# A two-layer trunk: modulation sums spread over other stages, the first head's inputs copied early, one norm per head

## The chip, the core and the metric

The kernel runs on one core of a Trainium2 chip. TensorE (PE) multiplies matrices and transposes tiles into PSUM, VectorE (DVE) and ScalarE (ACT) work on tiles and read PSUM, GpSimd (POOL) takes some work beside them, and SyncE's queue (SP) issues most of the transfers, in order. The metric is the time of one execution on the device in microseconds. The kernel before took 1466.41 us, the median of three runs (1465.34 to 1467.45).

## What is computed

A trunk of two layers over 1024 tokens of width 1024, in float32. Layer 0 is a gated delta rule in 8 heads, layer 1 is stick-breaking attention in 16 heads over keys and values that are computed once between the layers. Each layer's input is normed and modulated by vectors from `c`; the norm for keys and values has vectors of its own.

```python
for layer in range(DEPTH):
    mod = c_act @ w_ada[layer] + b_ada[layer]
    shift, scale, gate = mod[:, :D], mod[:, D:2 * D], mod[:, 2 * D:]
    h = _modulated_norm(x, norm_g[layer], shift, scale)
    if layer < N_A:
        y = _gdn_mixer(h, w_in_a[i], conv_w_a[i], a_log_a[i], dt_bias_a[i], o_gain_a[i], w_out_a[i])
    else:
        if layer == N_A:
            mkv = c_act @ w_ada_kv + b_ada_kv
            hk = _modulated_norm(x, kv_norm_g, mkv[:, :D], mkv[:, D:])
            kv = hk @ w_kv
...
        y = _sb_mixer(h, k_sh, v_sh, w_in_b[i], q_gain_b[i], w_out_b[i])
    x = x + (gate[:, None, :] * y).astype(x.dtype)
```

In the mixer of layer 0, queries, keys and values are projected, pass a causal convolution of four taps and a silu, queries and keys are normed, and a recurrence over chunks of 64 tokens runs per head. `beta` and the decay `g` ("the gates" below) come from 16 more columns of the projection. The recurrence's output is normed per head, multiplied by a silu of `z` and projected back.

## The kernel before

The work lies in four stages, and TensorE is the engine that all others feed.

**Start (0 to 78 us).** `x` is normed and transposed, the shift and scale of layer 0 are made, and the tokens times the gates' columns and the first head's queries go into PSUM (`ba_ps`, `q_ps`, L343 and L344). Then a block in which TensorE's order is that of the code (L439 to L497) projects the first head's keys into two banks (`pk0`), makes the gates from `ba` (sigmoid, exponentials, logarithm and a series, on tiles of 128x64 in a pool of their own, `gt`), sums them over the chunk with two matmuls (`pgc`, L484, L485), and transposes the sums (`pgt`, L493), which are written to memory and read back on all partitions.

**Heads (78 to 700 us).** `conv_silu` (L502) projects a head's queries or keys (for the first head it takes the finished ones out of PSUM), copies them from PSUM to `xp` (L512) and, scaled by one tap, to `qk` (L513), adds three taps on VectorE (L515) and applies the silu (L517). Each projection is three matmuls per block: every float32 operand is a high and a low half (`mm3`, L116 to L118; the weight's halves are `whi`, a cast on ScalarE, L211, and `wlo`, a subtract on VectorE, L212). `stage_qk` transposes (`ptk`, L543), squares (L545) and norms queries and keys, decays the keys (`kdec`, L549), makes the products of the chunk (`pgr`, L576) and inverts a triangular matrix row by row (L603, L606); `stage_c` (L688) runs the recurrence and norms its output, for each half of the tokens by a chain of 13 small VectorE operations (L735, L736 and `rsqrt`, L91). The loop over heads (L747) issues the next head's `stage_qk` ahead of the current head's rest. A scheduler orders the instructions of this stage, apart from the blocks said above to follow the code.

Two vectors of layer 0's and the key/value norm's and three of layer 1's are still missing: `mods` (L527) lists six pairs of matrix and part. After each of the heads 0 to 5, `mod_acc` (L145) sums one of them: sixteen loads of 256 KB (`mraw`) and sixteen VectorE operations on 128x512 (`macc`, L153, L155), and in the next head `mod_fin` (L170) transposes the sums (`pc`, L182) and adds them up by two ScalarE instructions for each transpose (L185).

**Keys and values (700 to 945 us).** The rest of layer 0 and the projection of keys and values, in TensorE's hand-written order (L947 on). `keys_values` goes through eight column blocks `n`, four of keys and then four of values, each in two halves of four steps; a step is 24 matmuls on 256 columns. After each block `mod_b(n)` (L919) reads a part of the normed `x`, modulates it for layer 1 on ScalarE and splits it into halves, the low one by GpSimd (L927).

**Layer 1 (945 us to the end).** Queries, attention and the last projection; the change does not touch it.

Of the kernel before, what the change touches and what calls it, by code (L numbers as in the profile page):

```python
# [17 lines left out]
EPS = 1e-6  # L18
# [4 lines left out]
def kernel(  # L23
# [146 lines left out]
    def mod_fin(pool, ps_pool, ps_tag, i, part, accs, j0=0, turned=False):  # L170

        t = pool.tile([P, ND], F32, name="mt", tag="mt", bufs=2)
# [262 lines left out]


    k_ps = [dd_pool.tile([P, 512], F32, name="pk0", tag="dd"), o_pool.tile([P, 512], F32, name="pk0", tag="po")]
    with tc.tile_pool(name="gt", bufs=1, side="right", reuse_waits="tile") as gt:
        order = tc.manual_schedule(engines={PE.engine})  # L439
        order.__enter__()  # L440
        ba = gt.tile([P, T], F32, name="ba")
# [10 lines left out]
        alb = gt.tile([P, 2, HA], F32, name="alb")  # L452
# [3 lines left out]
        y = gt.tile([P, HA, NC], F32, name="gy")  # L456
        V.tensor_tensor(out=y, in0=pbv[:, 8:16, :], in1=alb[:, 1, :][:, :, None].broadcast_to([P, HA, NC]),
                        op=ALU.add)
        u = gt.tile([P, HA, NC], F32, name="gu")
        V.scalar_tensor_tensor(out=u, in0=y, scalar=-1.0, in1=y, op0=ALU.mult, op1=ALU.min)  # L460
        S.activation(out=u, in_=u, func=AF.Exp)
        ea = gt.tile([P, HA], F32, name="ea")
        S.activation(out=ea, in_=alb[:, 0, :], func=AF.Exp)
        w1 = gt.tile([P, HA, NC], F32, name="gw1")
        S.activation(out=w1, in_=u, func=AF.Ln, bias=1.0)

        sr = gt.tile([P, HA, NC], F32, name="gsr")
# [6 lines left out]
        mk = gt.tile([P, HA, NC], F32, name="gmk")  # L474
# [19 lines left out]
        gT = gt.tile([64, P], F32, name="gT")  # L494
        V.tensor_copy(out=gT, in_=pgt[:64, :P])
        dma(out=gTd, in_=gT)
        order.__exit__(None, None, None)  # L497

    gdn_stack = ctx.enter_context(ExitStack())
    gp = gdn_stack.enter_context(tc.tile_pool(name="gp", bufs=1, side="right", reuse_waits="tile"))  # L500

    def conv_silu(h, part, dst):  # L502
        j = part * 8 + h
        ready = {0: q_ps, 8: k_ps}.get(j)
        if not ready:
            hi, lo = split_w(load_w(w_in_a[0][:, j * P:(j + 1) * P]), [P, ND, P], None, V)
        xp = gp.tile([P, 3 + T], F32, name="xp", tag="xp", bufs=2)
        V.memset(xp[:, 0:3], 0.0)
        for hf in range(TH):
            ps = ready[hf] if ready else project(hi, lo, hT, hf)  # L510
            sl = slice(hf * 512, hf * 512 + 512)
            S.copy(out=xp[:, 3 + hf * 512:515 + hf * 512], in_=ps)  # L512
            S.activation(out=dst[:, sl], in_=ps, func=AF.Copy, scale=ccol[:, 72 + j:73 + j])  # L513
# [13 lines left out]
    mods = [(0, 2), (2, 1), (2, 0), (1, 1), (1, 0), (1, 2)]  # L527

    def stage_qk(h):

        qk = gp.tile([P, 2, T], F32, name="qk", tag="qk", bufs=3)
# [156 lines left out]
    def stage_c(h, st):  # L688
# [37 lines left out]
        for hf in range(TH):  # L726
            cs = slice(hf * 4, hf * 4 + 4)
            osb = osbs[hf]
            so = gp.tile([P, 4], F32, name="so", tag="so")
            for i in range(4):  # L730
                sqo = gp.tile([P, P], F32, name="sqo", tag="sqo")
                S.activation(out=sqo, in_=osb[:, i], func=AF.Square, accum_out=so[:, i:i + 1])

            qe = gp.tile([P, 4], F32, name="qe", tag="qe")
            V.tensor_scalar(out=qe, in0=n2[:, 0, cs], scalar1=EPS, scalar2=EPS * P, op0=ALU.add, op1=ALU.mult)  # L735
            V.scalar_tensor_tensor(out=so, in0=so, scalar=1.0 / P, in1=qe, op0=ALU.mult, op1=ALU.add)  # L736
            ro = rsqrt(gp, so, 4, "ro")
            V.tensor_tensor(out=osb, in0=osb, in1=ro[:, :, None].broadcast_to([P, 4, P]), op=ALU.mult)
            pt = ch_pool.tile([P, 4, P], F32, name="pto", tag="ch")
            for i in range(4):  # L740
                PE.transpose(pt[:, i], osb[:, i], ident)
            V.scalar_tensor_tensor(out=szs[hf], in0=pt.rearrange("p a b -> p (a b)"), scalar=ogain,
                                   in1=szs[hf], op0=ALU.mult, op1=ALU.mult)
            dma(out=oTa[h, :, hf * 512:hf * 512 + 512], in_=szs[hf])
# [4 lines left out]
    for h in range(HA):  # L749
# [169 lines left out]
    def mod_b(n):  # L919
# [360 lines left out]
```

## Time and profile before

| | |
|---|---|
| median of three runs | 1466.41 us (1465.34 to 1467.45) |
| the profiled execution | 1462.12 us |
| its span | 1460.3 us |
| mean granted clock of TensorE | 0.985 of full |
| TensorE, VectorE, ScalarE, GpSimd busy | 1374.8, 1040.8, 760.6, 92.3 us |

A granted clock of 1 is 2.4 GHz, and 0.5 is 1.2 GHz; a stretch between the two has part of its time at each. Matmuls overlap, so the pace of a stream is read from the starts of two neighbours, and the time of one is longer than that. In brackets behind an instruction stands the idle time of its engine just ahead of it and what ended that.

### The profile page before, as it was taken

How to read it: one execution, taken by the hardware profiler on the slowest of the kernel's cores; microseconds unless marked ns; L12 is line 12 of the kernel's file. 1: busy time of each engine (PE TensorE's matmuls, PEld its weight loads, DVE VectorE, ACT ScalarE, POOL GpSimd, SP SyncE). 2: the span in 40 equal slices, each digit the busy share in tenths (PEclk: the TensorE clock that was granted, in tenths of full speed). 3: DMA queues.
4: the chain of work that ended last, by engine and by line, in shares of the span. 5: the costliest groups of instructions: out<-in, count | busy, mean ns of one | idle time of the engine just before them, and what ended most of it. 6: DMA issues, size and time to landing. Idle time of an engine off the chain costs nothing.

```text
span 1460.3 us, 23391 instructions
## 1 busy us (share of the span) xinstructions
PE 1374.8 (94%) x8603; PEld 1145.8 (78%) x8603; DVE 1040.8 (71%) x2459; ACT 760.6 (52%) x1614; POOL 92.3 (6%) x98
## 2 busy tenths in 40 slices
PE   4989999799999999999799999999999999998998
PEld 3567778578878777788689999788888888885676
DVE  3568698878778788954886610488888888989332
ACT  5656546446564646431784422366666666665110
POOL 1000000000000000000221011301011011000000
PEclk9999999799999999999999999999999999999999
DMA  9334324443444444444844433624233233234511
GB/s 316 107 107 124 89 51 120 123 137 84 142 108 133 108 137 134 148 127 162 301 160 159 160 131 116 181 73 116 54 101 106 69 105 87 84 84 131 174 59 56
DMA packets 168132, 181.15 MB, mean 124 GB/s; under 512 B 36617, under 2 KB 121426, under 8 KB 168018
## 3 DMA queue, kind: packets, MB, share of 16 engines
q1 hardware_dynamic: 165184, 171.17, 39.4%
q0 software_dynamic: 2432, 8.39, 1.6%
q8 instruction: 68, 1.11, 0.3%
q14 instruction: 46, 0.38, 0.1%
q10 hardware_dynamic: 402, 0.10, 0.0%
HBM read 140.22 MB, written 39.40 MB: 123 GB/s over the span
## 4 chain that ended last, share of the span: by engine, by line
PE 70%; DVE 18%; ACT 6%; DMA 3%; issue 2%; SPq 0%; ACTq 0%; DVEq 0%
PE pj L116 16%; PE pj L117 16%; PE pj L118 16%; DVE kp L1074 3%; PE ptw L1089 3%; PE pa L1114 2%; PE pa L1115 2%; PE pl L1069 1%; PE pl L1068 1%; PE pgr L576 1%; DVE qk L515 1%; DVE wl L1096 1%; DVE macc L155 1%; DMA mraw<-in_w_ada_dram 1%; PE pa L1111 1%
## 5 line engine op out<-in xcount | busy, mean ns | idle before, releaser
L118 PE MATMUL pj<-hT,wlo 128*128 128x512 f32 x496 | 203.0, 410 | 10.2 <-DVE wlo L212 10.2
L116 PE MATMUL pj<-hT,whi 128*128 128x512 f32 x496 | 205.4, 414 | 3.7 <-ACT qk L513 2.6
L117 PE MATMUL pj<-hT,whi 128*128 128x512 f32 x496 | 204.5, 412 | 0.0
L1074 DVE TENSOR_TENSOR_SCAN kp<-kp,stick 128x896 f32<-128x896 f32 (+7 forms) x128 | 179.1, 1401 | 3.9 <-ACT kp L1070 2.6
L1070 ACT ACTIVATE kp<-pl,nrq 128x512 f32<-128x512 f32 (+1 forms) x192 | 107.0, 580 | 48.6 <-PE pl L1069 39.9
L1094 ACT ACTIVATE wh<-ptw 128x512 fp32r<-128x512 f32 (+3 forms) x152 | 84.6, 557 | 67.4 <-PE ptw L1089 63.2
L118 PEld LDWEIGHTS pj<-hT,wlo 128*128 128x128 f32 x496 | 95.2, 192 | 27.6 <-DVE wlo L212 11.8
L116 PEld LDWEIGHTS pj<-hT,whi 128*128 128x128 f32 x496 | 95.2, 192 | 24.2 <-issue 3.7
L116 PE MATMUL pj<-hbT,whi 128*128 128x512 f32 x256 | 108.0, 422 | 0.0
L117 PEld LDWEIGHTS pj<-hT,whi 128*128 128x128 f32 x496 | 95.3, 192 | 15.8
L116 PE MATMUL pj<-wo,oh 128*128 128x512 f32 x256 | 103.8, 405 | 4.0 <-ACT oh L254 2.3
L117 PE MATMUL pj<-wo,oh 128*128 128x512 f32 x256 | 102.1, 399 | 0.0
L118 PE MATMUL pj<-wo,ol 128*128 128x512 f32 x256 | 101.3, 396 | 0.5 <-DVE ol L255 0.5
L117 PE MATMUL pj<-hbT,whi 128*128 128x512 f32 x256 | 101.2, 395 | 0.0
L118 PE MATMUL pj<-hbT,wlo 128*128 128x512 f32 x256 | 101.2, 395 | 0.0
L1089 PE MATMUL ptw<-ident,kp 128*128 128x128 f32 x576 | 91.6, 277 | 8.1 <-DVE wl L1096 5.5
L212 DVE TENSOR_TENSOR wlo<-wraw,whi 128x1024 fp32r<-128x1024 f32 x56 | 68.7, 1226 | 39.8 <-ACT whi L211 35.5
L211 ACT CAST whi<-wraw 128x1024 fp32r<-128x1024 f32 x56 | 59.1, 1055 | 72.1 <-PE pj L117 61.0
L1096 DVE SCALAR_TENSOR_TENSOR wl<-ptw,wh 128x512 fp32r<-128x512 f32 (+1 forms) x140 | 87.3, 624 | 8.1 <-ACT wh L1094 7.2
L1089 PEld LDWEIGHTS ptw<-ident,kp 128*128 128x128 f32 x576 | 68.4, 142 | 27.3 <-DVE wl L1096 12.0
L1114 PE MATMUL pa<-wh,vt 128*128 128x256 f32 (+1 forms) x280 | 78.5, 302 | 10.6 <-DVE o L1131 10.6
L116 PE MATMUL pj<-whi,hkT 128*128 128x256 f32 x256 | 73.2, 286 | 2.4 <-DVE x L265 1.6
(324 smaller groups left out, 3428.8 us busy)
## 6 DMA issues: line engine op xcount, KB each, us to landing
mraw<-in_w_ada_dram SPq DMA_DIRECT2D x96, 256.0 KB
wraw<-in_w_in_a_dram SPq DMA_DIRECT2D x32, 512.0 KB
mraw<-in_w_ada_kv_dram SPq DMA_DIRECT2D x32, 256.0 KB
xr<-x_dram SPq DMA_DIRECT2D x16, 512.0 KB
wraw<-in_w_kv_dram SPq DMA_DIRECT2D x16, 512.0 KB
kT_dram<-kt SPq DMA_DIRECT2D x32, 256.0 KB
wraw<-in_w_in_b_dram SPq DMA_DIRECT2D x16, 512.0 KB
Kh<-kT_dram SPq DMA_DIRECT2D x32, 256.0 KB
```

What stands on the lines that cost most here:

```text
L116: PE.matmul(ps, lh, rh, start=start, stop=False)
L117: PE.matmul(ps, lh, rl, start=False, stop=False)
L118: PE.matmul(ps, ll, rh, start=False, stop=stop)
L211: (copy or S.copy)(out=hi, in_=raw)
L212: (eng or G).tensor_tensor(out=lo, in0=raw, in1=hi, op=ALU.subtract)
L1070: S.activation(out=kp[:, s0:s0 + sw], in_=pl[:, :sw], func=AF.Sigmoid, scale=nrq[p][:, t, e:e + 1])
L1074: V.tensor_tensor_scan(out=kr, data0=kr, data1=stick[:, T - n:][:, ::-1], initial=1.0, op0=ALU.mult, op1=ALU.max)
L1089: PE.transpose(pt[:, i], kps[p, e, 2 * g + q][:, j * P:(j + 1) * P], ident)
L1094: S.activation(out=wh[:, :nb], in_=pt[:, :nb], func=AF.Copy, bias=-1.0)
L1096: V.scalar_tensor_tensor(out=wl[:, :nb], in0=pt[:, :nb], scalar=-1.0, in1=wh[:, :nb], op0=ALU.add, op1=ALU.subtract)
L1114: PE.matmul(dst, lh, wh[:, sl], start=(j == 0), stop=False)
L1115: PE.matmul(dst, lh, wl[:, sl], start=False, stop=(j == nj - 1))
```

## The change

1. The first head's queries and keys are copied from PSUM (`taps_in`) inside the gates' block, the queries ahead of the gates, each half of the keys behind its projection; `conv_silu` then finds them in `first_xp` and `first_qk`. The gates' tiles are pieces of one tile in the heads' pool, which is opened earlier. The block in which TensorE follows the order of the code stays; later work can still come in between.
2. `mods` keeps three pairs, and each of the heads 0 to 5 sums one half of one. Layer 1's three vectors are summed in the stage of keys and values, in twelve quarters of 256 columns (four loads of 256 KB and eight VectorE operations on 128x256 each), which begin at the steps `MOD_Q`, counted from block 4 on; a quarter is transposed four steps after it began.
3. `mod_b` goes from the end of each block to the steps `MOD_B`, and its low half is made by VectorE.
4. `stage_c` norms both halves of the tokens by one chain, but in the last head.

```diff
-    def mod_fin(pool, ps_pool, ps_tag, i, part, accs, j0=0, turned=False):
+    def mod_quarters(pool, i, part):
+
+        for n0 in range(0, D, 256):
+            src = mod_src[i][:, part * D + n0:part * D + n0 + 256].rearrange("(p k) n -> p k n", k=8)
+            acc = pool.tile([P, 256], F32, name="macq", tag=("of", "oh", "ol")[n0 // 256 % 3], bufs=2)
+            for k in range(0, 8, 2):
+                raw = pool.tile([P, 2, 256], F32, name="mrawq", tag="x2k", bufs=5)
+                dma(out=raw, in_=src[:, k:k + 2])
...
-        else:
+        elif js.stop == ND:
             pr = ps_pool.tile([P, 512], F32, name="pr", tag=ps_tag)
             PE.transpose(pr[:ND, :P], t, ident)
...
+    def taps_in(j, ps, hf, xp, dst):
+
+        S.copy(out=xp[:, 3 + hf * 512:515 + hf * 512], in_=ps)
+        S.activation(out=dst[:, hf * 512:hf * 512 + 512], in_=ps, func=AF.Copy, scale=ccol[:, 72 + j:73 + j])
...
+        for hf in range(TH):
+            taps_in(0, q_ps[hf], hf, first_xp[0], first_qk[:, 0])
...
         for hf in range(TH):
             project(hi, lo, hT, hf, k_ps[hf])
+            taps_in(8, k_ps[hf], hf, first_xp[1], first_qk[:, 1])
...
-    mods = [(0, 2), (2, 1), (2, 0), (1, 1), (1, 0), (1, 2)]
+    mods = [(0, 2), (2, 1), (2, 0)]
+    half_acc = []
...
+        groups = [(0, 1)] if h < HA - 1 else [(0,), (1,)]
+        for group in groups:
+            ga = slice(group[0] * 4, group[-1] * 4 + 4)
...
+            ro = rsqrt(gp, so[:, ga], 4 * len(group), f"ro{len(group)}")
...
-        if h < len(mods):
-            i, part = mods[h]
-            pend = (i, part, [mod_acc(gp, i, part, n0, 512, 2) for n0 in (0, 512)])
+        if h < 2 * len(mods):
+            i, part = mods[h // 2]
+            half_acc.append(mod_acc(gp, i, part, h % 2 * 512, 512, 2))
+            if h % 2:
+                pend, half_acc = (i, part, half_acc), []
...
-            G.tensor_tensor(out=hT[hf][:, 1, n], in0=xs, in1=hT[hf][:, 0, n], op=ALU.subtract)
+            V.tensor_tensor(out=hT[hf][:, 1, n], in0=xs, in1=hT[hf][:, 0, n], op=ALU.subtract)
...
+    def mods_b(step, made):
+
+        if quarters and quarters[0][0] + 4 <= step:
+            _, i, acc, j0 = quarters.pop(0)
+            mod_fin(kp_, wk_pool, "wk", 1, (1, 0, 2)[i], [acc], j0, tg if i == 2 else None, turned=True)
+        if step in MOD_Q:
+            n = MOD_Q.index(step)
+            quarters.append((step, n // 4, *next(made)))
...
+                    if n >= 4:
+                        mods_b(step, made)
+                        if step in MOD_B:
+                            mod_b(MOD_B.index(step))
+                        step += 1
                     yield
...
-            mod_b(n)
+    MOD_Q = (0, 1, 3, 4, 6, 7, 9, 10, 16, 19, 22, 25)
+    MOD_B = (15, 16, 18, 19, 21, 22, 24, 26)
```

ScalarE's order at the first head, before: `gu` and `gw` belong to the gates, `pgc` are their sums in PSUM, `pj` and `pk` the first head's queries and keys there.

```order
L465 ACTIVATE gw_681<-gu 128x64
L211 CAST whi<-wraw 128x1024
L490 ACT_TABLE_LOAD
L490 ACTIVATE gA_110<-pgc 128x64
L491 ACTIVATE gA_109<-gA_109 128x64
L512 COPY xp<-pj 128x512
L513 ACTIVATE qk<-pj,ccol 128x512
L512 COPY xp<-pj 128x512
L513 ACTIVATE qk<-pj,ccol 128x512
L512 COPY xp<-pk_597 128x512
L513 ACTIVATE qk<-pk_597,ccol 128x512
L512 COPY xp<-pk_598 128x512
```

And with the change, where `gsm` is the gates' tile:

```order
L478 COPY ba<-pba 128x512 x2
L457 COPY xp<-pj 128x512
L458 ACTIVATE qk<-pj,ccol 128x512
L457 COPY xp<-pj 128x512
L458 ACTIVATE qk<-pj,ccol 128x512
L493 ACT_TABLE_LOAD
L493 ACTIVATE gA_111<-pb 128x64
L501 ACT_TABLE_LOAD
L501 ACTIVATE gsm<-gsm 128x8
L633 COPY tt<-tinit 128x256
L227 CAST whi<-wraw 128x1024
L457 COPY xp<-pk_603 128x512
```

The copies of the queries have moved from behind the gates' last exponentials to ahead of their first (`pb`, the sigmoid); the first half of the keys (`pk_603`) follows its projection, ahead of the rest of the gates, and so does the second further down.

TensorE behind the keys of the first head (`pgc`: the gates' sums, `pj`: the second head's queries), before and, from that projection's seventeenth matmul, with the change:

```order
L117 MATMUL pk_598<-hT,whi 128x512
L118 MATMUL pk_598<-hT,wlo 128x512
L484 MATMUL pgc<-gw_681,tri 128x64
L485 MATMUL pgc<-gw_681,ones 128x64
L493 MATMUL pgt<-ident,gA_108 64x128
L116 MATMUL pj<-hT,whi 128x512
L117 MATMUL pj<-hT,whi 128x512
```

```order
L117 MATMUL pj<-hT,whi 128x512
L118 MATMUL pj<-hT,wlo 128x512
L116 MATMUL pj<-hT,whi 128x512
L117 MATMUL pj<-hT,whi 128x512
L522 MATMUL pgc<-gsm,tri 128x64
L523 MATMUL pgc<-gsm,ones 128x64
L118 MATMUL pj<-hT,wlo 128x512
L116 MATMUL pj<-hT,whi 128x512
L117 MATMUL pj<-hT,whi 128x512
L118 MATMUL pj<-hT,wlo 128x512
L116 MATMUL pj<-hT,whi 128x512
L531 MATMUL pgt<-ident,gA_108 64x128
```

The gates' sums and their transpose stood ahead of the second head's first projection (`pj`); with the change that projection follows the keys at once, and the sums come after twenty of its matmuls.

SyncE's queue at the eight quarters that come first, with the change, behind the last loads of the stage's weights:

```order
L177 DMA mrawq<-in_w_ada_dram 128x2x256 x5
L233 DMA wraw<-in_w_kv_dram 128x4x256
L177 DMA mrawq<-in_w_ada_dram 128x2x256
L233 DMA wraw<-in_w_kv_dram 128x4x256
L177 DMA mrawq<-in_w_ada_dram 128x2x256 x2
L958 DMA kT_dram<-kt 128x512 x3
L177 DMA mrawq<-in_w_ada_dram 128x2x256
L958 DMA kT_dram<-kt 128x512
L177 DMA mrawq<-in_w_ada_dram 128x2x256 x7
L941 DMA v_dram<-kv 128x4x128
L942 DMA v_dram<-kv 4x1x128
L941 DMA v_dram<-kv 128x4x128
```

And TensorE at the last quarter:

```order
L118 MATMUL pj<-kwh,hkT 128x256
L198 MATMUL pc<-ident,macq 128x128 x2
L218 MATMUL pr<-ident,tg 8x128
L116 MATMUL pj<-whi,hkT 128x256
L117 MATMUL pj<-wlo,hkT 128x256
```

Quarters' loads, two weights (`wraw`), the last key tiles (`kT_dram`) and the first values (`v_dram`) share the queue; on TensorE, `pr` is the very next instruction after the last quarter's transposes.

## Rows read from the trace of the kernel before

**Rows 1.** The page, part 1: busy us, share of the span, instructions.

```profile
PE 1374.8 (94%) x8603; PEld 1145.8 (78%) x8603; DVE 1040.8 (71%) x2459; ACT 760.6 (52%) x1614; POOL 92.3 (6%) x98
```

**Rows 2.** Busy time by stretch (busy us and instructions per engine, granted clock, DMA share, GB/s).

```profile
core 0: us, PE busy (x) PEld busy (x) DVE busy (x) ACT busy (x) POOL busy (x), PEclk, DMA share, GB/s
...
78.00:88.00 10.00, 7.02 (x22) 5.40 (x21) 4.74 (x10) 7.70 (x15) 0.00 (x0) 0.66 0.56 162
88.00:258.00 170.00, 167.34 (x1023) 135.25 (x1022) 143.83 (x442) 99.89 (x215) 0.00 (x0) 1.00 0.36 98
258.00:282.00 24.00, 13.89 (x45) 9.32 (x44) 23.24 (x87) 10.83 (x28) 0.00 (x0) 0.65 0.43 120
282.00:475.00 193.00, 191.06 (x1265) 155.42 (x1264) 151.18 (x493) 107.41 (x271) 0.00 (x0) 1.00 0.44 121
475.00:484.00 9.00, 6.03 (x23) 4.52 (x22) 9.00 (x30) 7.15 (x13) 0.00 (x0) 0.81 0.50 134
484.00:700.00 216.00, 209.51 (x1333) 169.32 (x1331) 154.57 (x483) 93.98 (x231) 1.46 (x3) 1.00 0.46 142
...
800.00:900.00 100.00, 100.00 (x858) 100.00 (x857) 34.22 (x59) 35.98 (x69) 14.23 (x10) 1.00 0.41 134
```

**Rows 3.** TensorE's waits, 100 to 700 (us in total, times, longest).

```profile
PE pj L118 <- DVE wlo L212: 10.2, 4, 5.4
PE pgr L576 <- ACT kdec L549: 3.2, 2, 1.6
```

**Rows 4.** TensorE's timeline at the first head (start us, us, instruction, idle before).

```profile
81.97 0.80 PE L116 MATMUL pj<-hT,whi 128*128 128x512 f32 x1 [2.57 <-ACT qk L513]
...
87.66 0.40 PE L117 MATMUL pj<-hT,whi 128*128 128x512 f32 x1
87.89 0.40 PE L118 MATMUL pj<-hT,wlo 128*128 128x512 f32 x1
...
93.29 1.09 PE L543 MATMUL ptk<-ident,qk 128*128 128x128 f32 x8 [1.15 <-ACT qk L517]
```

**Rows 5.** ScalarE's timeline at the first head.

```profile
78.13 1.04 ACT L211 CAST whi<-wraw 128x1024 fp32r<-128x1024 f32 x1 [6.90 <-PE pk L117]
...
80.75 0.58 ACT L512 COPY xp<-pj 128x512 f32<-128x512 f32 x1
...
82.27 0.72 ACT L513 ACTIVATE qk<-pj,ccol 128x512 f32<-128x512 f32 x1
```

**Rows 6.** TensorE's timeline, 255 to 285.

```profile
267.15 2.07 PE L576 MATMUL pgr<-qk 128*128 128x256 f32 x4 [1.61 <-ACT kdec L549]
...
276.04 0.79 PE L118 MATMUL pj<-hT,wlo 128*128 128x512 f32 x1 [5.39 <-DVE wlo L212]
```

**Rows 7.** VectorE's timeline, 247 to 283.

```profile
262.20 0.75 DVE L155 SCALAR_TENSOR_TENSOR macc<-mraw,cact,macc 128x512 f32<-128x512 f32 x1
...
274.77 1.21 DVE L212 TENSOR_TENSOR wlo<-wraw,whi 128x1024 fp32r<-128x1024 f32 x1
```

**Rows 8.** Groups of VectorE, 78 to 700 (busy us, mean ns, idle before).

```profile
L155 DVE SCALAR_TENSOR_TENSOR macc<-mraw,cact,macc 128x512 f32<-128x512 f32 x84 | 62.6, 745 | 6.3 <-DMA mraw<-in_w_ada_dram 4.5 <-DMA mraw<-in_w_ada_kv_dram 1.5
...
L101 DVE SCALAR_TENSOR_TENSOR ro_y<-ro_z,ro_y 128x4 f32<-128x4 f32 x48 | 7.5, 156 | 0.4
...
L153 DVE TENSOR_SCALAR macc<-mraw,cact 128x512 f32<-128x512 f32 x12 | 5.8, 481 | 9.5 <-ACT macc L185 9.5
```

**Rows 9.** The sums' groups on ScalarE and TensorE, 78 to 700.

```profile
L185 ACT ACTIVATE macc<-pc 128x128 f32<-128x128 f32 x48 | 12.5, 286 | 8.2 <-PE pc L182 8.2
...
L185 ACT ACTIVATION_READ_ACCUMULATOR macc<-pc 128x1 f32 x48 | 10.4, 217 | 0.0
...
L182 PE MATMUL pc<-ident,macc 128*128 128x128 f32 x48 | 7.3, 275 | 0.0
```

**Rows 10.** The DMA view, 0 to 40.

```profile
DMA packets 7758, 12.43 MB, mean 311 GB/s; under 512 B 1853, under 2 KB 3062, under 8 KB 7756
...
mraw<-in_w_ada_dram SPq DMA_DIRECT2D x32, 256.0 KB
```

More of the change, by code (lines that the diff above doesn't have):

```diff
@@ L168, in mod_rows, with mod_fin @@
         return row
-    def mod_fin(pool, ps_pool, ps_tag, i, part, accs, j0=0, turned=False):
-        t = pool.tile([P, ND], F32, name="mt", tag="mt", bufs=2)
+    def mod_quarters(pool, i, part):
[5 more added lines that the diff above has]
+                dma(out=raw, in_=src[:, k:k + 2])
+                for kk in range(2):
+                    if k + kk == 0:
+                        V.tensor_scalar(out=acc, in0=raw[:, 0], scalar1=cact[:, 0:1], scalar2=None, op0=ALU.mult)
+                    else:
+                        V.scalar_tensor_tensor(out=acc, in0=raw[:, kk], scalar=cact[:, k + kk:k + kk + 1], in1=acc,
+                                               op0=ALU.mult, op1=ALU.add)
+            yield acc, n0 // P
+    def mod_fin(pool, ps_pool, ps_tag, i, part, accs, j0=0, t=None, turned=False):
+        t = t if t is not None else pool.tile([P, ND], F32, name="mt", tag="mt", bufs=2)
         nj = accs[0].shape[1] // P
@@ L455 @@
         S.activation(out=beta, in_=pbv[:, 0:8, :], func=AF.Sigmoid)
-        y = gt.tile([P, HA, NC], F32, name="gy")
+        y = small_tile(P, [HA, NC])
         V.tensor_tensor(out=y, in0=pbv[:, 8:16, :], in1=alb[:, 1, :][:, :, None].broadcast_to([P, HA, NC]),
                         op=ALU.add)
-        u = gt.tile([P, HA, NC], F32, name="gu")
+        u = small_tile(P, [HA, NC])
         V.scalar_tensor_tensor(out=u, in0=y, scalar=-1.0, in1=y, op0=ALU.mult, op1=ALU.min)
         S.activation(out=u, in_=u, func=AF.Exp)
-        ea = gt.tile([P, HA], F32, name="ea")
+        ea = small_tile(P, [HA])
         S.activation(out=ea, in_=alb[:, 0, :], func=AF.Exp)
-        w1 = gt.tile([P, HA, NC], F32, name="gw1")
+        w1 = small_tile(P, [HA, NC])
         S.activation(out=w1, in_=u, func=AF.Ln, bias=1.0)
-        sr = gt.tile([P, HA, NC], F32, name="gsr")
+        sr = small_tile(P, [HA, NC])
         coef = [-1.0 / 6, 1.0 / 5, -1.0 / 4, 1.0 / 3, -1.0 / 2, 1.0]
@@ L473 @@
         V.tensor_tensor(out=sr, in0=sr, in1=u, op=ALU.mult)
-        mk = gt.tile([P, HA, NC], F32, name="gmk")
+        mk = small_tile(P, [HA, NC])
         V.tensor_scalar(out=mk, in0=u, scalar1=0.02, scalar2=None, op0=ALU.is_lt)
@@ L493 @@
         PE.transpose(pgt[:64, :P], f(gcum), ident)
-        gT = gt.tile([64, P], F32, name="gT")
+        gT = small_tile(64, [P])
         V.tensor_copy(out=gT, in_=pgt[:64, :P])
         dma(out=gTd, in_=gT)
-        order.__exit__(None, None, None)
-    gdn_stack = ctx.enter_context(ExitStack())
-    gp = gdn_stack.enter_context(tc.tile_pool(name="gp", bufs=1, side="right", reuse_waits="tile"))
     def conv_silu(h, part, dst):
         j = part * 8 + h
-        ready = {0: q_ps, 8: k_ps}.get(j)
-        if not ready:
+        if j in (0, 8):
+            xp = first_xp[part]
+            V.memset(xp[:, 0:3], 0.0)
+        else:
             hi, lo = split_w(load_w(w_in_a[0][:, j * P:(j + 1) * P]), [P, ND, P], None, V)
[L507 to L513, printed above, removed]
+            xp = gp.tile([P, 3 + T], F32, name="xp", tag="xp", bufs=2)
+            V.memset(xp[:, 0:3], 0.0)
+            for hf in range(TH):
+                taps_in(j, project(hi, lo, hT, hf), hf, xp, dst)
         for w in range(3):
@@ L724, in stage_c @@
             osbs.append(osb)
[L726 to L744, printed above, removed]
@@ L926, in mod_b, with sums_of_mods @@
             V.tensor_copy(out=hT[hf][:, 0, n], in_=xs)
-            G.tensor_tensor(out=hT[hf][:, 1, n], in0=xs, in1=hT[hf][:, 0, n], op=ALU.subtract)
+            V.tensor_tensor(out=hT[hf][:, 1, n], in0=xs, in1=hT[hf][:, 0, n], op=ALU.subtract)
+    tg = kp_.tile([P, ND], F32, name="tg", bufs=1)
+    quarters = []
+    def sums_of_mods():
+        for part in (1, 0, 2):
+            yield from mod_quarters(kp_, 1, part)
+    def mods_b(step, made):
[5 more added lines that the diff above has]
+            quarters.append((step, n // 4, *next(made)))
     def keys_values():
-        parts, tail = kv_weights(0), None
+        parts, tail, made, step = kv_weights(0), None, sums_of_mods(), 0
         yield
```

40 lines of the change are left out of this document (34 added, 6 removed).

## The prediction

> **What bounds the kernel now.** I read the page's first part, then the busy time of each engine by stretch, then the waits of TensorE in the heads' stage, and last the instructions at the two worst stretches.
>
> TensorE is busy for 1374.8 of 1460.3 us [rows 1]. The question is therefore where it is not, and where it runs at half clock. The table by stretch gives both [rows 2]. From 88 to 258 it is idle for 170 − 167.34 = 2.7 us, from 282 to 475 for 1.9, from 484 to 700 for 6.5: near its limit. Three stretches stand out. From 78 to 88 the granted clock is 0.66 and 3.0 us are idle. From 258 to 282 the clock is 0.65, 10.1 us are idle, and VectorE is busy for 23.24 of 24. From 475 to 484 the clock is 0.81, 3.0 us are idle, and VectorE is busy for 9.00 of 9. From 800 to 900 TensorE has no gap, while VectorE is busy for 34 and ScalarE for 36 of 100.
>
> The view of waits names the cause in the heads [rows 3]: 10.2 us in four waits for `wlo`, the low half of a weight that VectorE makes, 5.4 the longest, and 3.2 for `kdec`. So two things cost time between 78 and 700: the hand-over after the first head's projections, and VectorE falling behind.
>
> **The change, part by part.** All sums are against the profiled execution, 1462.12 us (span 1460.3); it lies 4.3 below the median of the runs, 1466.41.
>
> *First head, queries and keys out of PSUM early.* In the trace TensorE's next projection starts at 81.97 after 2.57 us of waiting for ScalarE's copy of the queries [rows 4]. ScalarE had been idle for 6.90 us until 78.13; then come a weight's cast, a table load and two exponentials, and only at 80.75 to 82.99 the four copies of q [rows 5]. The copies sat behind the gates in the queue, not behind data. Now they stand ahead of the gates there, and the projection's weight is cast during the keys' projection. It can start right after the keys, near 78.4 (the cast at 78.13 was released by the last matmul but one of the keys [rows 5]); the three gate matmuls (0.4 us) follow inside it. Worth 81.97 − 78.4 − 0.4 = 3.1 us. The pause also left the clock at 1.2 GHz: from 81.97 to 87.66 fourteen matmuls start, 5.7 us, where one takes 0.23 at full clock [rows 4], so 5.7 − 3.2 = 2.5 us more. The transposes at 93.29 waited 1.15 for the silu, which now runs early. Together 6.75. The new queue is full: table load, silu and the keys' copies share ScalarE with the gates, and VectorE's three keys' convolutions stand between the gates' last steps. Walking the order with row durations, the gate matmul comes due about when its operand does, with a few tenths to spare. I take −6; bounds −6.75 and 0.
>
> *VectorE's load in the heads.* Out go 48 of 96 sums: 42 at 0.745 and 6 at 0.481 us, 34 us [rows 8]; ScalarE loses 24 pairs at 0.286 + 0.217, 12 us [rows 9]. The merged norm saves thirteen small operations in each of seven heads; at the 0.156 us of `ro_y` [rows 8], 14 us of record and less of occupancy. This falls on the stretches where VectorE is late. In 258 to 282 `wlo` runs at 274.77, and VectorE works without a gap before it; a sum at 262.20 is one of those ahead [rows 7]. Halving the sums and norms between 247 and 275 takes some 8 us out of the queue ahead of a wait of 5.39 [rows 6], and `kdec` stands in ScalarE's queue behind squares whose buffer VectorE's reductions free. The loss of the stretch is 10.1 us idle, and half clock for (1 − 0.65) × 2 × 24 = 16.8 us, in which 5.39 + 1.61 = 7.0 are idle [rows 6]; the 9.8 of work there cost 4.9 extra. Of these 15.0 I take −13. From 475 to 484: 3.0 idle, 9 × 0.19 = 1.7 of clock; I take −4. The other two waits for `wlo` (4.8 − 3.0 = 1.8 [rows 3]): −1.5. Bounds: nothing, if other waits come in their place, and all idle time and clock between 88 and 700, 24.2 + 6.6 = 30.8 us [rows 2].
>
> *What arrives in the K/V stage.* 96 sums on 128x256, bounded by the 0.745 of twice the width and the 0.156 of four columns [rows 8]; at 0.4, about half of the first, 38 us on VectorE, and 12 us on ScalarE. Both have over 60 us free from 800 to 900 alone [rows 2], so they cost nothing. That cover has a limit in order: TensorE's order is fixed by hand, and each quarter's two transposes stand four steps after its loads. A step is 24 matmuls at 100/858 us [rows 2], 2.8 us. Walked step by step, each sum ends some 5 us before. The 24 transposes are as many as leave the heads [rows 9]; they lie on the path there as here, net 0. Twelve switches between small and large matmuls cost about 0.1 us each, 1. The last quarter's `pr` transpose follows at once on a round trip over ScalarE's two accumulating pairs (2 × 0.5 [rows 9]) and VectorE; TensorE waits: +2, between 1 and 4 with a clock drop.
>
> *mod_b.* Sixteen subtracts on 128x512 leave GpSimd for VectorE, 12 us at the 0.745 of such an operation [rows 8]; hidden by the same cover. Its loads come later, but end before the queries of the next layer by steps 26 to 31.
>
> *DMA.* From the first quarter's load to the eighth's last stand 32 pieces of 256 KB, two weights, four key tiles and two pairs of value stores in SP's queue: 8.4 + 1.05 + 1.05 + 1.05 = 11.5 MB in about fourteen steps, 39 us, 295 GB/s. The stage moves 134 now [rows 2]; but the first 40 us of the kernel ran at a mean of 311, with 32 such pieces among the loads [rows 10]. The margin is thin, yet the sums start some steps ahead. I put it at nothing.
>
> Sum: −6 − 13 − 4 − 1.5 + 1 + 2 = −21.5. 1462.1 − 21.5 = 1440.6; plus 4.3: **1445**.
>
> **Rivals.**
>
> *A. The waits only move.* The order in the heads is made anew, and another engine (ScalarE, the `kdec` chain, the `bf` DMA) is next. For it: `kdec` and others already wait in the same stretch [rows 3]. Against: without 48 us VectorE is well ahead. Only the first head and a third of 18.5 remain: −6 − 6 + 3 = −9, 1457.
>
> *B. VectorE no longer holds anything up.* All 30.8 and 6.75 go, less the 3 given back, 34.5: 1432. Against: some idle time lies in the chains of the recurrence.
>
> *C. Slower: the sums arrive late in the K/V stage.* TensorE's queue is in order, so every late quarter stops it, where there is no gap today [rows 2]. The price is 11.5 MB over the rate, less 39 us: at the 159 to 134 GB/s that this stage has shown, 72 to 86 us, 33 to 47 late: 1478 or more after the gain. It decides below 11.5/(39 + 24.4) = 181 GB/s, where the time ends 2.9 above the median. Against it the 311 of [rows 10]. The Trainium skill speaks for it (DMA: Bandwidth & Descriptors, section on measured bandwidth): transfers want 1 MiB for 75% of the peak, and one of 64 KB reaches 138 GB/s. By its fit of 2.0 us and the bytes at 436 GB/s, estimated, a piece alone takes 2.6 us, 32 of them 83 us, 44 late, and the sum would be 1489. The trace disagrees where several pieces are in flight: 32 of them, with other loads, took 40 us [rows 10], and five buffers serve the quarters.
>
> *D. The early copies don't help.* A sum of gates' vectors stands in VectorE's queue between the gates' steps and waits for its load; if that is late, gate matmul and head wait as now: first term 0, 1451.
>
> **How the numbers follow.** Forecast with its neighbours (1437 to 1451, D's 0.1 within) 0.63; A 0.17; B 0.09; C 0.07; no net effect 0.04. The forecast's own range is 1437 to 1452; with A inside, and half of B, the range is 1432 to 1459. A measurement of this kernel can tell about 0.2%, 2.9 us, from no change: faster 0.87, same 0.05, slower 0.08.
>
> **What would show it.** After the change: the first `pj` within 0.5 us of the last `pk`, clock 1.00 from 78 to 88; `ptk` of the first head near 87 to 90, not 93 to 97; no wait for `wlo` over 1 us before 700, and the heads' stage shorter by some 24 us and its 24 transposes; in the K/V stage one wait of 1 to 2 us at `pr`, none over 0.5 at `pc`. Wrong would be: waits at `pc` for `macq` (C), a clock below 1 somewhere new between 100 and 690 (A), or a first projection that still waits.

## The result and the profile after

| | before | after |
|---|---|---|
| median, four runs each | 1466.93 us (1465.34 to 1469.04) | 1440.29 us (1439.12 to 1445.16) |
| span of the profiled execution | 1460.3 us | 1437.4 us |

The change takes 1.75% off: the ratio is 0.9825, 95% interval 0.9807 to 0.9844. The forecast was 1445, in a range of 1432 to 1459. The time by stretch, in the stretches of [rows 2] as far as the shorter heads allow:

```profile
core 0: us, PE busy (x) PEld busy (x) DVE busy (x) ACT busy (x) POOL busy (x), PEclk, DMA share, GB/s
0.00:78.00 78.00, 56.66 (x290) 35.98 (x291) 37.13 (x88) 45.64 (x72) 6.09 (x22) 0.91 0.61 205
78.00:88.00 10.00, 10.00 (x47) 8.33 (x46) 9.10 (x24) 6.65 (x10) 0.00 (x0) 1.00 0.43 126
...
250.00:282.00 32.00, 31.60 (x231) 25.22 (x230) 24.22 (x75) 21.20 (x57) 0.00 (x0) 1.00 0.32 88
...
475.00:484.00 9.00, 9.00 (x71) 7.26 (x70) 1.84 (x5) 4.82 (x13) 0.00 (x0) 1.00 0.35 97
...
800.00:900.00 100.00, 92.87 (x774) 91.52 (x774) 70.00 (x161) 34.80 (x96) 1.45 (x5) 0.98 0.81 251
```

The reader sees three things. The stretch from 78 to 88 has no idle time and a clock of 1.00, where [rows 2] had 3.0 us idle at 0.66. The stretches from 250 to 282 and from 475 to 484 are full, 31.60 of 32 and 9.00 of 9, with the clock at 1.00. And from 800 to 900, where TensorE had no gap, it is now idle for 7.1 us, with the clock at 0.98 and the DMA engines busy for 0.81 of the time, against 0.41.

The first head in TensorE's timeline:

```profile
81.86 0.39 PE L118 MATMUL pk<-hT,wlo 128*128 128x512 f32 x1
82.09 0.39 PE L116 MATMUL pj<-hT,whi 128*128 128x512 f32 x1
...
86.63 0.33 PE L522 MATMUL pgc<-gsm,tri 128*128 128x64 f32 x2
...
94.05 0.60 PE L577 MATMUL ptk<-ident,qk 128*128 128x128 f32 x4
```

The second head's projection (`pj`) starts one matmul after the keys' last, the gates' sums (`pgc`) come without a wait, and the last of the first head's sixteen transposes of queries and keys (`ptk`; the line at 94.05 stands for four, the last of them at 94.4) starts 12.5 us behind the keys' last matmul. Three of TensorE's waits in the heads, from 78 to 690, as in [rows 3]:

```profile
PE pgr L610 <- ACT kdec L583: 1.5, 1, 1.5
PE pto L780 <- DVE osb L777: 1.1, 3, 0.5
...
PE pgr L610 <- DVE nm L615: 0.7, 2, 0.5
```

No wait for `wlo` is left among the eleven lines of that view; before, it had 10.2 us. And the stage of keys and values, the waits at the quarters' transposes and at `pr`:

```profile
822.34 0.44 PE L198 MATMUL pc<-ident,macq 128*128 128x128 f32 x2 [0.91 <-DVE macq L182]
...
825.91 0.44 PE L198 MATMUL pc<-ident,macq 128*128 128x128 f32 x2 [0.33 <-DVE macq L182]
...
833.20 0.44 PE L198 MATMUL pc<-ident,macq 128*128 128x128 f32 x2 [1.26 <-DVE macq L182]
...
838.97 0.62 PE L198 MATMUL pc<-ident,macq 128*128 128x128 f32 x2 [2.54 <-DVE macq L182]
```

```profile
895.18 0.27 PE L218 MATMUL pr<-ident,tg 128*8 128x128 f32 x1 [0.97 <-DVE tg L209]
```

Four of the twelve quarters were late, by 5.0 us together, and `pr` waited 0.97.

**Where the time went.** Four marks on TensorE cut each trace: the keys' last matmul (`pk`), the last of the first head's sixteen transposes, the first transposes of the next stage (`ptx`) and layer 1's first projection (`hbT`). The starts of these, in the trace before, stand at 77.9, 97.6, 698.8 and 920.4, after the change at 81.9, 94.4, 666.2 and 900.9:

| stretch | before | after | difference |
|---|---|---|---|
| start, to the keys' last matmul | 77.9 | 81.9 | +3.9 |
| first head | 19.7 | 12.5 | −7.2 |
| rest of the heads | 601.2 | 571.9 | −29.3 |
| keys and values | 221.5 | 234.7 | +13.2 |
| layer 1, to the last matmul | 534.6 | 531.2 | −3.4 |

The first and the last line are not counted as the change's: the runs below, in which TensorE has the same work there, have 77.6 to 84.3 and 530.9 to 534.3 (the 534.6 before lies just outside). So the change wins 36.5 us in the heads and gives 13.2 back.

### The profile page after: what moved, and what is told of

Read it like the earlier page. It is cut to its first block, busy times and chain, and to the rows that moved or that the text cites. A ratio compares the mean times of both kernels' runs of the same rounds, so it can differ in the third digit from the quotient of the medians.

```text
span 1437.4 us, 23380 instructions
## 1 busy us (share of the span) xinstructions
PE 1365.7 (95%) x8603; PEld 1143.0 (80%) x8603; DVE 1059.4 (74%) x2447; ACT 762.4 (53%) x1614; POOL 69.7 (5%) x82
## 4 chain that ended last, share of the span: by engine, by line
PE 66%; DVE 19%; DMA 7%; ACT 6%; issue 2%; SPq 0%; POOL 0%; ACTq 0%; DVEq 0%; POOLq 0%
PE pj L116 14%; PE pj L117 14%; PE pj L118 14%; DVE kp L1138 4%; PE ptw L1153 3%; DMA mrawq<-in_w_ada_dram 2%; PE pa L1178 2%; PE pa L1179 2%; DVE qk L548 1%; PE pl L1133 1%; PE pl L1132 1%; PE pgr L610 1%; DVE wl L1160 1%; DVE macq L182 1%; PE pw L741 1%
## 5 line engine op out<-in xcount | busy, mean ns | idle before, releaser
L116 PE MATMUL pj<-hT,whi 128*128 128x512 f32 x496 | 203.2, 410 | 0.9 <-ACT sz L665 0.9
L117 PE MATMUL pj<-hT,whi 128*128 128x512 f32 x496 | 201.5, 406 | 0.0
L1153 PEld LDWEIGHTS ptw<-ident,kp 128*128 128x128 f32 x576 | 68.0, 141 | 28.2 <-DVE wl L1160 12.6
```

What stands on the lines that cost most here:

```text
L116: PE.matmul(ps, lh, rh, start=start, stop=False)
L117: PE.matmul(ps, lh, rl, start=False, stop=False)
L1153: PE.transpose(pt[:, i], kps[p, e, 2 * g + q][:, j * P:(j + 1) * P], ident)
```

## The experiments

Each run is an edit of the changed kernel, apart from what is said; each is compared with the kernel before on the same chip. The three columns of stretches are read from one trace each, at the marks above. The kernel before took 1466.93 us beside the changed kernel and 1467.73 to 1469.53 beside the others, so medians of different rows compare to some 3 us only.

| run | median us (lowest to highest) | first head | rest of heads | keys, values |
|---|---|---|---|---|
| changed kernel | 1440.29 (1439.12 to 1445.16) | 12.5 | 571.9 | 234.7 |
| copies late | 1447.08 (1446.14 to 1447.95) | 12.5 | 580.2 | 233.7 |
| sums in heads | 1447.50 (1444.89 to 1449.32) | 12.5 | 591.2 | 223.3 |
| norm in halves | 1443.06 (1439.97 to 1445.83) | 12.5 | 574.5 | 236.3 |
| one load for a quarter | 1432.46 (1431.11 to 1435.87) | 12.5 | 573.5 | 227.4 |
| quarters even | 1442.96 (1440.73 to 1443.67) | 12.5 | 573.7 | 233.7 |
| first head only | 1459.79 (1449.59 to 1464.99) | 12.5 | 597.9 | 224.7 |
| own pool | 1452.40 (1450.92 to 1454.54) | 19.6 | 577.0 | 233.1 |
| dummy sums | 1438.10 (1434.13 to 1439.42) | 12.5 | 573.8 | 234.4 |
| sums without loads | 1433.99 (1430.76 to 1436.05) | 17.2 | 573.2 | 222.7 |
| sums by ones | 1450.04 (1443.47 to 1451.20) | 12.5 | 586.8 | 224.4 |
| quarters even, early loads | 1442.89 (1441.39 to 1446.55) | 12.5 | 574.2 | 234.9 |
| sums by GpSimd's queue | 1467.88 (1465.25 to 1473.54) | 12.5 | 611.9 | 222.2 |

### The first head

*Copies late:* the copies go back behind the gates in the code.

```diff
-        for hf in range(TH):
-            taps_in(0, q_ps[hf], hf, first_xp[0], first_qk[:, 0])
...
-            taps_in(8, k_ps[hf], hf, first_xp[1], first_qk[:, 1])
...
             V.memset(xp[:, 0:3], 0.0)
+            for hf in range(TH):
+                taps_in(j, (q_ps if part == 0 else k_ps)[hf], hf, xp, dst)
```

> The changed kernel with the first head's copies put back behind the gates (the gates' tiles stay in the heads' pool). My theory: the early copies are worth what the first head lost, the gap of 4 us between the keys' last matmul and the next projection, 2.5 us of half clock and a wait of 1.2: about 7 us, 1447 against 1440, the whole difference before the third group of key transposes, the rest of the heads within 3 us of the changed kernel. Rival (the shift only re-times everything behind it): under 2 us, or over 12 with stalls later in the heads.

1447.08, as expected, and for another reason. The first head takes 12.5 us here too: the scheduler took the copies forward by itself. The 6.8 us were lost behind it, in 580.2 against 571.9 us of the rest, spread over waits in the recurrence and the triangular rows:

```profile
PE pS L745 <- DVE vv L742: 2.9, 2, 1.7
...
PE pgr L609 <- DVE nm L614: 1.7, 3, 0.8
PE py L696 <- DVE tb L691: 1.1, 2, 0.9
```

So my number was right by luck and my theory of this run wrong. The mechanism is the rival's, though not its size: what moves at the head re-times the stage behind, by 8.3 us in this pair.

*Own pool:* the gates' tiles in a pool `gt` that closes ahead of the heads' pool, and the copies behind, as before the change; the sums, the norm and `mod_b` stay changed.

```diff
+    with tc.tile_pool(name="gt", bufs=1, side="right", reuse_waits="tile") as gt:
+        ba = gt.tile([P, T], F32, name="ba")
...
-    gsm = gp.tile([P, 512], F32, name="gsm", tag="e1")
-            taps_in(8, k_ps[hf], hf, first_xp[1], first_qk[:, 1])
```

> The changed kernel without the first part: the gates' tiles in a pool of their own that closes ahead of the heads' pool, the copies behind. The run with the copies alone put back kept them early, so what held them may be the memory that the two pools shared. If so, the gap of 4 us, the half clock and the wait come back here: 7 us, 1446 to 1449. If the copies stay early here too, the pool is not the cause and the gap stays under 1 us.

The old head came back, with the waits of [rows 4], 2.57 us to the hundredth and 0.98 for 1.15; below TensorE's lines stands ScalarE's, with the idle time of [rows 5]:

```profile
80.90 0.40 PE L118 MATMUL pk<-hT,wlo 128*128 128x512 f32 x1
...
84.94 0.80 PE L116 MATMUL pj<-hT,whi 128*128 128x512 f32 x1 [2.57 <-ACT qk L529]
...
96.12 1.09 PE L560 MATMUL ptk<-ident,qk 128*128 128x128 f32 x8 [0.98 <-ACT qk L533]
```

```profile
81.10 1.04 ACT L227 CAST whi<-wraw 128x1024 fp32r<-128x1024 f32 x1 [6.90 <-PE pk L117]
```

19.6 us against 12.5. What had put the copies late was the gates' pool: `xp` and `qk` belong to a pool that opened only when it closed. With the shared pool the copies came early from either place in the code, so where the tiles lived decided. Whether the memory itself held them, or the order that the scheduler made when the pool opened (in both old heads they stand behind this weight's cast), the runs do not separate. The medians are 12.1 us apart, and the other 5 lie in the rest of the heads, 577.0.

*First head only:* the kernel before with this part of the change alone; six whole vectors in the heads, `mod_b` after each block with GpSimd's subtract, the norm in halves.

```diff
-    mods = [(0, 2), (2, 1), (2, 0)]
+    mods = [(0, 2), (2, 1), (2, 0), (1, 1), (1, 0), (1, 2)]
...
-        groups = [(0, 1)] if h < HA - 1 else [(0,), (1,)]
+        groups = [(0,), (1,)]
...
-    MOD_Q = (0, 1, 3, 4, 6, 7, 9, 10, 16, 19, 22, 25)
-    MOD_B = (15, 16, 18, 19, 21, 22, 24, 26)
+    MOD_Q = ()
+    MOD_B = ()
```

> The kernel before with the first part of the change alone (gates' tiles in the heads' pool, the first head's copies early). My theory: the first head's 7 us and nothing else, 1458 to 1461, with the waits for the weights' low half in the heads as before. Rival (the early head re-times the whole stage): the heads change by more than 5 us either way behind the first 20 us.

1459.79, a ratio of 0.9935 (0.9908 to 0.9961): the head's 7.2 us, and the waits for `wlo` are all there.

```profile
PE pj L118 <- DVE wlo L228: 9.3, 4, 5.7
PE pgr L609 <- ACT kdec L582: 4.2, 4, 1.7
```

### What the sums cost in the heads

*Sums in heads:* the list of six pairs and the whole vector after each head come back, and no quarters; `mod_b`, norm and first head stay changed.

```diff
-            half_acc.append(mod_acc(gp, i, part, h % 2 * 512, 512, 2))
+            pend = (i, part, [mod_acc(gp, i, part, n0, 512, 2) for n0 in (0, 512)])
...
-    MOD_Q = (0, 1, 3, 4, 6, 7, 9, 10, 16, 19, 22, 25)
+    MOD_Q = ()
```

> The changed kernel with layer 1's three vectors summed in the heads again, one whole vector after each of the heads 0 to 5; mod_b, the merged norm and the early copies stay as changed. My theory (VectorE's load made it late in the heads): 20 to 27 us come back in the heads with waits for the weights' low half, and the stage of keys and values gets its 12 us back: 1450 to 1456. Rival (it was the norm's chain of small operations, or the new order as such): the heads move by less than 5 us, so the time falls to 1430 to 1434.

The heads take 19.4 us more, a little under the 20 to 27 of my theory, and keys and values 11.4 less, which leaves 8.0. The median rose by 7.2, less than the 10 I had expected at least. The rest of the heads has waits for `wlo` again (2.0 us in three) and some in the recurrence. So moving the sums is worth about 8 us net, and of the heads' gain it is the larger part.

*Dummy sums:* is it VectorE's time? Eight more operations on 128x512 after each of six heads.

```diff
             half_acc.append(mod_acc(gp, i, part, h % 2 * 512, 512, 2))
+            for _ in range(8):
+                V.scalar_tensor_tensor(out=half_acc[-1], in0=half_acc[-1], scalar=0.0, in1=half_acc[-1],
+                                       op0=ALU.mult, op1=ALU.add)
```

> The changed kernel with eight more VectorE operations on 128x512 after each of the heads 0 to 5, on the finished sum (times 0 plus itself, so its value stays): the VectorE time of the sums that left, about 35 us, without their loads, transposes and ScalarE's work. If VectorE's load made the heads late, 10 to 20 us come back: 1450 to 1460, with waits for the weights' low half. If the loads, ScalarE or the new order as such did it, under 4 us.

Here my theory fell. The groups of VectorE in the heads, and the busy time of a stretch in which VectorE carries as much as before:

```profile
L816 DVE SCALAR_TENSOR_TENSOR macc<-macc 128x512 f32<-128x512 f32 x48 | 32.8, 684 | 0.1
...
L155 DVE SCALAR_TENSOR_TENSOR macc<-mraw,cact,macc 128x512 f32<-128x512 f32 x40 | 29.9, 747 | 7.7 <-DMA mraw<-in_w_ada_kv_dram 4.9 <-DMA mraw<-in_w_ada_dram 2.6
```

```profile
88.00:664.00 576.00, 568.13 (x3620) 462.18 (x3618) 465.35 (x1415) 314.85 (x710) 1.46 (x3) 1.00 0.38 106
```

```profile
88.00:664.00 576.00, 554.28 (x3531) 446.67 (x3530) 465.04 (x1490) 312.17 (x742) 0.00 (x0) 0.98 0.42 117
```

VectorE is busy for 465.35 us here and for 465.04 in the kernel before (the third column of the two, behind TensorE's), and TensorE's share is 568.13 against 554.28. 32.8 us of VectorE's time came back, and the rest of the heads took 1.9 us more. VectorE's load as such was not what cost. One limit remains: these operations need no data from outside, so the scheduler was freer to place them than sums that wait for loads.

*Sums without loads:* the run "sums in heads" with one load for each half vector; seven of eight loads are left out, VectorE's sums, transposes and ScalarE's pairs stay.

```diff
-            raw = pool.tile([P, wide], F32, name="mraw", tag="mraw", bufs=raw_bufs)
-            dma(out=raw, in_=src[:, k])
             if k == 0:
+                raw = pool.tile([P, wide], F32, name="mraw", tag="mraw", bufs=raw_bufs)
+                dma(out=raw, in_=src[:, 0])
```

> The run with the sums in the heads, with one load for each half vector in place of eight, all eight operations reading it; 84 of 96 loads are left out, so the summed vectors are not the reference's. Adding VectorE time alone cost nothing, so what cost 19 us in the heads there is the loads (waited for at the head of VectorE's queue, and standing in SyncE's) or the adding-up (ScalarE's pairs, transposes, PSUM banks). If the loads: the heads come down by 10 us or more to 584 to 593, total 1430 to 1438. If the adding-up: the heads stay at 598 to 604, total 1444 or more.

The rest of the heads falls by 18.0 us, from 591.2 to 573.2, but the first head takes 4.7 more: its order was drawn anew, and 64 matmuls of the second head's projections lie in it, where most runs have 44. The two stretches together fall by 13.4, from 603.8 to 590.4, and the changed kernel has 584.4. So of the 19.4 us that the sums cost in the heads, 13.4 went with the loads, and 6.0 stay with the adding-up, the sums and the order. The loads are the larger part, with the reserve that a new order alone moved 8.3 us above.

*Sums by ones:* "sums in heads" with the adding-up by matmuls on a column of ones, without transposes and ScalarE's pairs.

```diff
-            mod_fin(gp, wk_pool, "wk", *pend, turned=True)
+            mod_fin(gp, wk_pool, "wk", *pend)
```

> The run with the sums in the heads, with each sum added up by matmuls with a column of ones in place of transposes and ScalarE's pairs: 48 pairs, 24 us of ScalarE, leave the heads; the loads and VectorE's sums stay. If the adding-up is what cost: the heads come down by 10 us or more, total 1431 to 1437. If the loads: the heads move by less than 4 us, total 1443 to 1448.

The rest of the heads takes 4.4 us less, just outside both of my ranges, and the median of 1450.04, with runs from 1443.47, is no lower. The adding-up is at most a small part.

*Sums by GpSimd's queue:* how do the loads cost? SyncE's queue is in order, and weights and triangular rows stand behind the loads of sums. Here these loads leave it.

```diff
-            dma(out=raw, in_=src[:, k])
+            G.dma_start(out=raw, in_=src[:, k])
```

> The run with the sums in the heads, with the 96 loads issued from GpSimd's queue in place of SyncE's; the loads, VectorE's sums and the adding-up all stay in the heads. If the loads cost by standing in SyncE's queue ahead of the weights and of the triangular rows (its waits at them were 130 us there, 168 before the change, 82 after it): the heads come down by 10 us or more to 584 to 593, and with the stage of keys and values at 223 the total is 1428 to 1436, faster than the changed kernel. If they cost by their traffic or by VectorE waiting for them: the heads stay at 598 or more, 1443 or more.

The opposite came out: 611.9 us in the rest of the heads, and the time of the kernel before, ratio 1.0007 (0.9995 to 1.002). The sums' group on VectorE in three runs, the idle time ahead of it in the last columns; first "sums in heads", then "sums without loads", then this one:

```profile
L155 DVE SCALAR_TENSOR_TENSOR macc<-mraw,cact,macc 128x512 f32<-128x512 f32 x82 | 61.3, 748 | 6.1 <-DMA mraw<-in_w_ada_dram 4.9 <-DMA mraw<-in_w_ada_kv_dram 0.7
```

```profile
L156 DVE SCALAR_TENSOR_TENSOR macc<-mraw,cact,macc 128x512 f32<-128x512 f32 x84 | 59.1, 748 | 0.3
```

```profile
L155 DVE SCALAR_TENSOR_TENSOR macc<-mraw,cact,macc 128x512 f32<-128x512 f32 x84 | 63.0, 751 | 55.7 <-DMA mraw<-in_w_ada_dram 34.0 <-DMA mraw<-in_w_ada_kv_dram 20.9
```

VectorE stood idle for 6.1, 0.3 and 55.7 us ahead of the sums, in the first and the last nearly all of it for loads, and the heads from the first to the last took 603.8, 590.4 and 624.4. VectorE takes its queue in order: a sum without its load holds up `vv` of the recurrence, for which TensorE waits. In the last run that is 13.8 us at one line:

```profile
PE pS L745 <- DVE vv L742: 13.8, 10, 3.4
```

This shows that late loads cost through VectorE's queue. It does not settle what the loads cost in SyncE's: from GpSimd's queue each landed 3.0 us after its issue (the median) with two buffers to land in, and this lateness can hide a gain at SyncE. Nor does it show that the 6.1 us of "sums in heads" make all of its 13.4: the dummy sums' run waits 7.7 us for loads and loses 1.9, so where the waits fall in the order decides as much. How the 13.4 divide between these waits, SyncE's queue, the traffic and the order stays open.

### The norm

```diff
-        groups = [(0, 1)] if h < HA - 1 else [(0,), (1,)]
+        groups = [(0,), (1,)]
```

> The changed kernel with the norm of each head in two halves again. My theory: the chain's thirteen small operations per head occupy VectorE for 1 to 2 us, which has room now: 0 to 5 us more, 1440 to 1445. Rival (the chain is what held the heads up): 10 us or more, 1450 or higher.

1443.06, 2.6 us more in the rest of the heads: in the expected band, and hardly more than the runs' spread. The rival is out.

### The stage of keys and values

*One load for a quarter:*

```diff
-                raw = pool.tile([P, 2, 256], F32, name="mrawq", tag="x2k", bufs=5)
-                dma(out=raw, in_=src[:, k:k + 2])
+                if k == 0:
+                    raw = pool.tile([P, 2, 256], F32, name="mrawq", tag="x2k", bufs=5)
+                    dma(out=raw, in_=src[:, 0:2])
```

> The changed kernel with one load for each quarter of layer 1's sums in place of four, all eight sums reading it: the modulation of layer 1 is then not the reference's; 9.4 MB of loads are left out. If the 5 us of waits for the sums come from the transfers (rival C of the prediction in small), they vanish, and with them the clock's drop near 850: 5 to 8 us less, 1432 to 1435. If they come from VectorE's queue, the waits stay and the time is within 2 us of the changed kernel.

Of four loads for a quarter this run has one. The median is 7.8 us lower, and in the trace this stage is 7.3 shorter. TensorE's waits in it hold no `macq` any more, and the stretch that was idle for 7.1 us at a DMA share of 0.81 has:

```profile
800.00:900.00 100.00, 97.75 (x800) 95.76 (x800) 65.94 (x160) 35.66 (x98) 1.47 (x5) 1.00 0.55 169
```

TensorE is idle for 2.3 us there at a share of 0.55, with VectorE doing the same sums. So the waits came from transfers: rival C of the prediction, in small. In the changed kernel, from 798 to 906, VectorE (DVE) waited for the quarters' loads, and SyncE's queue (SPq), ahead of such a load, for a sum to free one of the five buffers:

```profile
DVE macq L182 <- DMA mrawq<-in_w_ada_dram: 7.9, 7, 1.7
DVE macq L180 <- DMA mrawq<-in_w_ada_dram: 6.9, 5, 3.3
```

```profile
SPq L177 <- DVE macq L182: 19.4, 26, 3.0
```

No run has more buffers or larger pieces, so whether the rate of the DMA engines, the five buffers or the size of the pieces made the loads late is not shown.

*Quarters even:* could the same loads be spread? Twelve quarters over the steps 0 to 25, `mod_b` from step 9.

```diff
-    MOD_Q = (0, 1, 3, 4, 6, 7, 9, 10, 16, 19, 22, 25)
-    MOD_B = (15, 16, 18, 19, 21, 22, 24, 26)
+    ORDER_Q = [(0,), (1,)] * 4 + [(2,)] * 4
+    MOD_Q = (0, 2, 4, 6, 8, 11, 13, 15, 18, 20, 22, 25)
+    MOD_B = (9, 10, 13, 14, 18, 19, 22, 23)
...
-        if quarters and quarters[0][0] + 4 <= step:
+        if quarters and quarters[0][0] + 5 <= step:
```

> The changed kernel with the twelve quarters spread evenly over the steps 0 to 25, scale and shift of the same columns in turn, each transposed five steps after it began, and mod_b as its columns come ready (steps 9 to 23). If the waits for the sums come from 8 quarters' loads crowded into the first fourteen steps, they fall below 1 us in total and the stage of keys and values gives back 5 to 8 us: 1432 to 1436. If the stage's transfers are too much wherever they stand, waits of 3 us or more remain: 1438 or higher.

No wait for `macq` is left, and the stage is 1.0 us shorter, no more. TensorE now waits for the copies of the values, and ScalarE, which makes them, stood in front of loads of `mod_b`, for 13.3 us (in the changed kernel it was 11.3, with 3.4 the longest); first TensorE's waits, then ScalarE's:

```profile
PE pj L116 <- ACT kv L930: 4.1, 4, 2.3
```

```profile
ACT xhl L964 <- DMA xhl<-xhT_dram: 13.3, 4, 4.9
```

*Quarters even, early loads:* `mod_b`'s loads four steps ahead of their use, and `pr` two steps behind its last sum; some of the later quarters and `mod_b` also move by one or two steps.

```diff
+                        if step + 4 in MOD_B:
+                            mod_b_load(MOD_B.index(step + 4))
...
+                        if step == 30:
+                            gate_out(kp_, wk_pool, "wk", 1, tg)
```

> The evenly spread quarters once more, with mod_b's loads issued four steps ahead of their use and the gate's transpose one step after its sum. There ScalarE stood 4.9 us in front of such a load and the copies of the values behind it were late. If that was the stage's loss, no wait over 1 us stays in the steps of the values, and the stage gives back 5 to 9 us against the changed kernel: 1431 to 1436. If the transfers are too many wherever they stand, waits of 3 us or more in total stay: 1438 or higher.

234.9 us: nothing gained. The next load in line was late, a weight that ScalarE casts, and the copies of the values behind it:

```profile
PE pj L116 <- ACT kv L935: 8.8, 3, 7.5
```

```profile
ACT whi L232 <- DMA wraw<-in_w_kv_dram: 6.8, 1, 6.8
```

`pr`'s wait went, as meant. So it is not the crowding of eight quarters: with 12.6 MB more in this stage some load was late in each of the three orders tried. Of the runs that keep every load, none beats the changed kernel clearly. The dummy sums' 1438.10 is 2.2 us lower, but the start of that trace is 2.8 shorter, its ratio of 0.9786 (0.9757 to 0.9814) overlaps the changed kernel's, and its edit only adds work.

`mod_b`'s move (part 3 of the change) has no run of its own. Four runs have it without the quarters, and their stage takes 222.2 to 224.4 us; "first head only", with the old `mod_b`, takes 224.7. No cost of it is seen.

## Why the prediction was right

- **First head:** forecast −6, with 6.75 as the sum; measured −7.2 in the trace, 12.5 us in place of 19.7. The three losses that the sum named are each gone, the gap, the clock and the wait at the first transposes, and the gates' sums came in time, as the walk had said. "The copies sat behind the gates in the queue, not behind data" is what the trace shows, but not the cause: the gates' pool put them there, and moving them in the code was not what the change needed.
- **VectorE's load in the heads:** forecast −18.5 and the 24 transposes; measured −29.3. The places were right: the two stretches that [rows 2] showed are full, and `wlo` is waited for nowhere. The size was between the forecast and the bound of 30.8 (rival B): about 2 of the 29.3 are the transposes that left (four take 0.35 us to the next matmul, in either trace). The step that failed is "Halving the sums and norms between 247 and 275 takes some 8 us out of the queue" as the reason for the gain: VectorE's time came back in the dummy sums' run at a price of 1.9 us. What counted of the sums were mostly their loads, 13.4 of 19.4 us in one pair of runs, up to what the order does.
- **K/V stage:** forecast +1 and +2, with the transposes net 0; measured +13.2. "Each sum ends some 5 us before" failed: four sums ended after their transposes were due. `macq` 5.0, `pr` 1.0 (taken as 2) and the values' copies 1.1 make 7.1 of idle time. The rest is the transposes that were booked against the heads (0.14 us from a pair to the next matmul, 1.7 for twelve), the forecast 1 for the switches, and time at half clock, some of it behind the longest wait: from 840 to 860 the granted clock was 0.94. The term "DMA" that was put "at nothing" is the one that was mis-sized, by the 7.3 us that went with the loads. A sum of a quarter also took 0.48 us, where 0.4 was taken.
- **The trace and the rule:** the estimate from the fit in the Trainium skill (DMA: Bandwidth & Descriptors, Anatomy of one DMA), 44 us late, did not come; the page gives that fit for transfers issued from GpSimd, and these are issued from SyncE. The nothing that I took did not come either. The stretch of 800 to 900 moved 251 GB/s at a DMA share of 0.81, below the 295 that the sum asked of the first fourteen steps. The 311 GB/s of [rows 10] was the wrong witness: its pieces have the same 256 KB, but its packets are longer, with 3062 of 7758 under 2 KB, while the changed kernel has, from 800 to 860:

```profile
DMA packets 16813, 15.48 MB, mean 258 GB/s; under 512 B 905, under 2 KB 16066, under 8 KB 16807
```

What shorter packets cost, no run here shows.

- **The whole:** the heads won 12 us more than forecast and keys and values lost 10 more, some 2 of each being the 24 transposes. The signs are opposite, so the profiled execution came out at 1439.12 for a forecast of 1440.6, in part by luck. The median is 5 us under its forecast, mostly since the changed kernel's profiled execution lies 1.2 below its median and not the 4.3 that was added. Of the signs, the early head, the clock and `wlo` came as said, and so did one sign of being wrong, the waits at `pc` for `macq`. Right in sign and size of the whole, then, and less so in its parts.

## What to carry to other kernels

A busy engine next to a stall is not yet its cause: give it its work back without the transfers, and see whether the stall returns. Work that waits for a load holds up everything behind it on an in-order engine, so it is moved to where its loads are early, not to where the engine is idle. And where a tile's pool opens only when another closes, look at the pool first: here moving the copies in the code changed nothing at the first head, and moving the tiles did.

## What the runs showed of the hardware

The start of the program, up to the keys' last matmul, has the same work for TensorE in all runs and ended between 77.6 and 84.3 us. It goes with the clock: in three traces that ended it at 77.6 to 78.0 the granted clock of the first 78 us was 0.98, in six that ended it at 81.8 to 83.5 it was 0.91. The other five had 0.96 at 78.5 and 79.1, 0.93 at 80.9 and 81.2, and 0.89 at 84.3. What sets it stays open: the run "one load for a quarter", whose start is the changed kernel's code, had 77.6, and the changed kernel 81.9. A difference of 4 us between two single executions says nothing about an edit here; lengths of stages within a trace say more, up to the 8.3 us by which a new order alone moved one.
